# First modulations in chunks of 128 features, with norm and six open sums following chunk by chunk

## The chip, the cores and the metric

One core of one Trainium2 chip runs the whole program in a single launch. The metric is the time of one execution on the device in microseconds (us), as the median of several runs.

## What is computed

A two-layer backbone over 1024 latent tokens and 256 context tokens with 1024 features. The part of the reference that the change touches is the beginning of the first layer:

```python
for l in range(DEPTH):                                   # DEPTH = 2
    m_lat = (silu(c) @ w_mod[l] + b_mod[l])              # 6 modulations of 1024 features, latent tokens
    m_ctx = (silu(c_ctx) @ w_mod[l] + b_mod[l])          # the same for context tokens
    sh1, sc1, ga1, sh2, sc2, ga2 = split(m_lat, 6)       # shift, scale, gate; twice
    ...
    pl = modulate(rms_norm(x, g_mix[l]), sh1, sc1) @ w_in[l]       # modulate(h) = h * (1 + scale) + shift
    pc = modulate(rms_norm(ctx, g_mix[l]), csh1, csc1) @ w_in[l]
    # columns of w_in: A Mamba-2 SSD, B RG-LRU, C global attention, D windowed attention
    ...                                                  # mixers, w_out, gated residual, MLP, gated residual
```

All arithmetic is float32. Products of two large operands are made with three matmuls of split operands (high times high, high times low, low times high).

## The kernel before

**Layout.** Activations lie with features on the 128 partitions and tokens along the free axis; 1024 features are 8 tiles (k = 0 to 7). Tokens come in three groups: the 256 context tokens, latent tokens 0 to 511, and latent tokens 512 to 1023 (the third group). `h` is the normalised and modulated activation, held as a high part `hh` and a low part `hl`. `mm3` (L138) writes the three matmuls of one split product; its lines are L141, L142 and L143, whoever calls it. `act` (L133), `copy_a` (L130) and `stt` (L136) are helpers in the same way.

**The units.** A unit is one key/value head of an attention group. `unit_half` (L466) loads and splits half of its weights (8 tiles of 128 features by 256 columns; 264 for the first unit, which carries the 8 columns of the SSD's dt), and `unit_proj` (L485) makes its projection: 10 sums of 128 tokens each, 24 matmuls a sum.

**The start, in `run` (L1523).** `setup` loads constants and computes `csil`, the SiLU of both conditioning vectors, and per-layer parameters (`layer_params`, L186, which has a softplus of some 14 small VectorE instructions per layer). Then x is loaded, except the latent part of tiles 4 to 7 (the third group), and `norm_stats` (L365) squares it on ScalarE, adds the squares on VectorE, and lets TensorE sum over partitions with 2 + 4 matmuls against a column of ones. `mod_bank` (L306) computes 2048 columns of the modulations (bank 0: the first shift and scale) as one sum over 8 tiles of `w_mod`, 16 loads of 512 KB and 32 matmuls of 32 x 512, four side by side in four column groups of the array; four transposes then bring the result to feature layout. Only after the last of the 16 loads are shifts and scales known, and only then does `norm_apply` (L391) make `h`, tile by tile, and the first unit's matmuls follow.

**The rest of the layer.** `layer` (L1411) weaves generators by hand-set costs: first the unit C0 together with the third group's norm and with bank 1 of the modulations (`fill[0]`, 16 more loads of 512 KB into 3 landing buffers `e`), then attention of C0 with the first SSD projection (`p_ssd(0)`), and so on.

**What sets the order.** A scheduler places the instructions on each engine by priority (the order of the code) and by its own estimate of when an operand is ready; each engine then executes its list strictly in that order. All loads of the start are issued by one queue, SP, in order; a load into a landing buffer waits there for the last reader of that buffer, and everything behind it waits too. Landing buffers: `raw` 2, `e` 3, `u` 25 (shared with x and h).

PSUM has eight banks: `pm` 2, `qk` 3, `pt` 2, `po` 1.

## Time and profile before

| | us |
|---|---|
| median of 3 runs | 3107.39 (3104.77 to 3107.77) |
| the profiled execution | 3102.39 |
| its span, first to last instruction | 3100.6 |
| TensorE (PE) busy | 2972.3 (96% of the span) |
| VectorE (DVE) busy | 2195.9 (71%) |
| ScalarE (ACT) busy | 1516.4 (49%) |
| GpSimd (POOL) busy | 800.6 (26%) |
| mean granted TensorE clock | 0.988 |

TensorE is the engine that works nearly all the time. Its idle time is what a change can remove, and the place to look is the table of busy time by stretch: one stretch of 100 us, the first, holds more idle time of TensorE than any other. Matmuls of one engine overlap in the records (a matmul's duration includes its way through the array), so the price of one in a row of many is the distance between starts, not the duration. A float32 matmul that is not split leaves two records, a split one leaves one.

### The profile page before, as it was taken

Reading aid. Unit: us, or ns where it says so; the run is one execution under the profiler, and the core shown is the slowest. Engines: PE = TensorE matmul, PEld = TensorE weight load, DVE = VectorE, ACT = ScalarE, POOL = GpSimd, SP = SyncE. Lnnn points to the kernel's source line nnn. Section 1 sums busy time; section 2 is a strip of 40 time slices with the busy share of each in tenths; the row PEclk is TensorE's granted clock in tenths of the full one; section 3 lists DMA queues with packets and bytes.
Section 4 is the critical chain, followed back from the end, with each engine's and each line's share of the span. In section 5 each row is a group of like instructions: output and inputs, shape, how many; then the busy total and the mean of one; then the engine's idle time right before and its main releaser. Section 6 shows DMA issues by size and latency. Waiting matters only on the chain.

```text
span 3100.6 us, 45540 instructions
## 1 busy us (share of the span) xinstructions
PE 2972.3 (96%) x16210; PEld 2458.7 (79%) x16210; DVE 2195.9 (71%) x4385; ACT 1516.4 (49%) x3570; POOL 800.6 (26%) x708
## 2 busy tenths in 40 slices
PE   5998998989999999999999999999899999999999
PEld 2788887788889887788888688887788778778887
DVE  5778777787742656577777777778787886667775
ACT  4675776676544444321112577676675544442120
POOL 2214123241454100222111512223342510032220
PEclk9999998999999999999999999999999999999999
DMA  8200012330355545642222400112422564553231
GB/s 283 64 18 25 20 37 72 98 138 33 125 168 157 177 152 182 218 146 85 77 84 78 147 18 18 28 40 70 140 82 71 171 205 138 166 179 104 87 104 62
DMA packets 241076, 330.71 MB, mean 107 GB/s; under 512 B 37328, under 2 KB 159824, under 8 KB 240848
## 3 DMA queue, kind: packets, MB, share of 16 engines
q1 hardware_dynamic: 213200, 281.64, 28.5%
q10 hardware_dynamic: 27648, 46.15, 4.0%
q8 instruction: 128, 2.10, 0.3%
q14 instruction: 100, 0.82, 0.1%
HBM read 253.28 MB, written 74.45 MB: 106 GB/s over the span
## 4 chain that ended last, share of the span: by engine, by line
PE 58%; DVE 5%; ACT 4%; DMA 2%; POOL 2%; issue 2%; ACTq 0%; SPq 0%; POOLq 0%; DVEq 0%
PE qk L143 8%; PE qk L142 8%; PE qk L141 8%; PE pm L143 6%; PE pm L141 6%; PE pm L142 6%; PE pt L142 3%; PE pt L143 3%; PE pt L141 3%; PE pt L718 1%; DVE u L136 1%; PE po L727 1%; POOL wl L246 1%; PE po L728 1%; DMA u<-in_w_ffn 1%
## 5 line engine op out<-in xcount | busy, mean ns | idle before, releaser
L246 POOL TENSOR_TENSOR wl<-raw,wh 128x512 fp32r<-128x512 f32 (+1 forms) x224 | 318.8, 1437 | 1215.9 <-ACT wh L130 916.5
L141 PE MATMUL pm<-u,wh 128*128 128x512 f32 (+1 forms) x1271 | 473.8, 373 | 4.1 <-DVE u L136 2.8
L143 PE MATMUL pm<-u,wl 128*128 128x512 f32 (+1 forms) x1271 | 467.5, 368 | 1.3 <-POOL wl L246 1.3
L142 PE MATMUL pm<-u,wh 128*128 128x512 f32 (+1 forms) x1271 | 466.5, 367 | 0.0
L130 ACT ACTIVATE wh<-raw 128x512 fp32r<-128x512 f32 (+1 forms) x224 | 135.6, 628 | 484.2 <-PE qk L142 159.8
L143 PE MATMUL qk<-u,wl 128*128 128x512 f32 (+1 forms) x874 | 326.7, 374 | 1.0 <-POOL wl L246 1.0
L141 PE MATMUL qk<-u,wh 128*128 128x512 f32 (+1 forms) x874 | 324.5, 372 | 1.9 <-DVE b L1342 1.0
L130 ACT ACTIVATE s<-pt 128x512 fp32r<-128x512 f32 (+4 forms) x548 | 251.2, 467 | 120.2 <-PE pt L718 74.4
L142 PE MATMUL qk<-u,wh 128*128 128x512 f32 (+1 forms) x810 | 300.2, 371 | 2.2 <-POOL u L409 1.8
L136 DVE SCALAR_TENSOR_TENSOR u<-pm,mods,u 128x512 f32<-128x512 f32 (+1 forms) x313 | 216.5, 693 | 90.4 <-PE pm L143 89.2
L141 PEld LDWEIGHTS pm<-u,wh 128*128 128x128 f32 x1271 | 243.1, 191 | 41.2 <-DVE u L136 4.4
L143 PEld LDWEIGHTS pm<-u,wl 128*128 128x128 f32 x1271 | 242.6, 191 | 35.4 <-POOL wl L246 2.7
L142 PEld LDWEIGHTS pm<-u,wh 128*128 128x128 f32 x1271 | 243.1, 191 | 30.8
L136 DVE SCALAR_TENSOR_TENSOR u<-qk,mods,u 128x512 f32<-128x512 f32 (+1 forms) x294 | 203.7, 693 | 84.2 <-PE qk L143 83.4
L133 ACT ACTIVATE b<-b 128x512 f32<-128x512 f32 (+4 forms) x256 | 146.1, 571 | 154.6 <-DVE b L1346 123.4
L133 ACT ACTIVATE e<-qk,t 128x512 f32<-128x512 f32 (+2 forms) x336 | 188.3, 571 | 42.3 <-DVE t L651 27.2
L722 DVE TENSOR_TENSOR s<-pt,s 128x512 fp32r<-128x512 f32 (+1 forms) x256 | 166.8, 661 | 39.7 <-ACT s L130 37.2
L1394 DVE TENSOR_TENSOR u<-e,u 128x256 fp32r<-128x256 f32 (+1 forms) x160 | 160.3, 1019 | 48.8 <-ACT u L130 27.6
L141 PEld LDWEIGHTS qk<-u,wh 128*128 128x128 f32 x874 | 165.2, 189 | 34.3 <-ACT u L130 1.7
L143 PEld LDWEIGHTS qk<-u,wl 128*128 128x128 f32 x874 | 164.6, 188 | 31.7 <-POOL wl L246 1.8
L141 PE MATMUL pm<-wh,u 128*128 128x256 f32 (+1 forms) x592 | 177.8, 301 | 3.3 <-ACT b L133 1.7
L142 PEld LDWEIGHTS qk<-u,wh 128*128 128x128 f32 x810 | 152.9, 189 | 31.3 <-POOL u L409 2.7
(325 smaller groups left out, 7526.3 us busy)
## 6 DMA issues: line engine op xcount, KB each, us to landing
raw<-in_w_ffn SPq DMA_DIRECT2D x184, 256.0 KB, 2.9
e<-in_w_mod SPq DMA_DIRECT2D x64, 512.0 KB, 4.5
u<-in_w_ffn SPq DMA_DIRECT2D x60, 512.0 KB, 5.1
m<-b ACTq DMA_DIRECT2D x96, 256.0 KB, 2.0
e<-m SPq DMA_DIRECT2D x32, 640.0 KB, 4.3
u<-in_w_mod SPq DMA_DIRECT2D x32, 512.0 KB, 6.3
e<-m SPq DMA_DIRECT2D x32, 512.0 KB, 3.9
raw<-in_w_in SPq DMA_DIRECT2D x48, 256.0 KB, 2.9
```

The costliest lines, as they stand in the source:

```text
L130: return self.nc.scalar.activation(o, i, AF.Copy, **k)
L133: self.nc.scalar.activation(o, i, fn, **k)
L136: self.nc.vector.scalar_tensor_tensor(o, a, s, b, op0=op0, op1=op1)
L141: mm(o, ah, bh, start=start, stop=False, skip_group_check=part)
L142: mm(o, ah, bl, start=False, stop=False, skip_group_check=part)
L143: mm(o, al, bh, start=False, stop=stop, skip_group_check=part)
L246: self.nc.gpsimd.tensor_sub(l, raw, f(h))
L718: nc.tensor.transpose(pt[:, e * 256 + hd * P:e * 256 + hd * P + P], prs[hd][0][:, (i + e) * P:(i + e) * P + P], self.ident)
L722: nc.vector.tensor_sub(tl, pt[:, :w], f(th))
L727: nc.tensor.matmul(po[:, :256], V[:, kc, :], th[:, c], start=i + e == 0, stop=False)
L728: nc.tensor.matmul(po[:, :256], V[:, kc, :], tl[:, c], start=False, stop=i + e == len(kcs) - 1)
L1394: self.nc.vector.tensor_sub(al[:, t], raw[:, t], f(ah[:, t]))
```

## The change

1. `csil` is laid out with 32 columns per tile (two used, 30 zero), so that a slice of 32 columns holds one tile's two vectors and nothing else.
2. The weights of all units (`wu` for C0 of both layers, `wv` for the other three) are laid out by the host so that one `raw` load is one contiguous run per partition, where it was three or four strided loads.
3. The part of `w_mod[0]` for bank 0 is laid out by the host as `wm`: chunk k holds, for all 1024 inputs, the 128 shift and 128 scale columns of feature tile k (2 loads of 512 KB).
4. A new function `begin` takes the place of the start in `run`. The statistics add the squares over tiles in PSUM: 16 + 32 matmuls against the column of ones, and no adds on VectorE. For each chunk, `mod` makes 8 matmuls of 32 x 256 (inputs in four column groups, two rounds), `mod_sum` adds the four groups by 2 small matmuls against `four`, VectorE adds the bias and makes the scale, `apply` makes tile k of `h` for context and the first latent group, and `proj` adds tile k to six sums of the first unit, held open in six PSUM banks. The third group's norm (`last`) is advanced inside the same loop from chunk 4 on. Chunks 5 to 7 land in the 3 buffers `e`.
5. `unit_proj` takes these six sums and makes the remaining four itself.
6. Most of `layer_params` moves from `setup` to the point behind the first weave of layer 0.

```diff
+        for k in range(3):
+            load(k)
+        rss = [stats(*g) for g in G_ALL[:2]]
+        rb = {g[0]: rows(g[1], rs) for g, rs in zip(G_ALL[:2], rss)}
+        nt = (CTX + 512) // P
+        self.sums = [self.PS(t)[:, :WU] for t in ("pm", "pm", "qk", "qk", "qk", "po")]
...
+        rest = last()
+        for k in range(KD):
+            if k + 3 < KD:
+                load(k + 3)
+            if k == 1:
+                for i in range(4, KD):
+                    nc.sync.dma_start(x.tiles[i][:, 0:1024], xt[i][:, 0:1024])
+            sb = mod(k)
+            if k >= 2:
+                proj(k - 2)
+            mod_sum(k, sb)
+            for g in G_ALL[:2]:
+                apply(k, *g)
+            if k >= 4:
+                for _ in range(5):
+                    next(rest, None)
...
+        proj(KD - 2)
+        proj(KD - 1)
...
+            for kk in range(KD):
+                cg = kk % 4
+                mm(ps[32 * cg:32 * cg + 32, 0:256], self.csil[:, 32 * kk:32 * kk + 32],
+                   land[k][kk // 4][:, 256 * cg:256 * cg + 256], start=kk < 4, stop=kk >= 4, skip_group_check=True,
+                   tile_position=(0, 32 * cg))
...
+            for k in range(KD):
+                sq, xk = self.S(n), x.at(k, t0, n)
+                if k % 2:
+                    nc.vector.tensor_mul(sq, xk, xk)
+                else:
+                    self.act(sq, xk, AF.Square)
+                for j in range(nt):
+                    mm(pss[:, j:j + 1], sq[:, j * P:(j + 1) * P], self.one, start=False, stop=k == KD - 1,
+                       skip_group_check=True)
...
+        def proj(k):
+            wh, wl = ws[k // 4]
+            for tt in range(nt):
+                self.mm3(self.sums[tt], hh.at(k, tt * P, P), hl.at(k, tt * P, P), wh[:, k % 4], wl[:, k % 4],
+                         k == 0, k == KD - 1, True)
...
         def loads(r, i):
...
+            c = (4 * kh + 2 * i) * nw
+            return [(r, w[:, c:c + 2 * nw])]
```

**TensorE at the start.** In these rows `pt`, `po`, `pm` and `qk` are PSUM banks, `one` is the column of ones, `s` a square or a copied modulation, `rnd` the identity, `csil` the conditioning, `u` and `e` landing buffers of `w_mod`, and `wh`, `wl` the split weights. Before:

```order
L384 MATMUL pt<-one,s 128x1 x2
L319 MATMUL po<-u,csil 32x512
L384 MATMUL pt<-one,s 128x1 x4
L319 MATMUL po<-u,csil 32x512 x3
L400 MATMUL pt<-rnd,t 128x128 x4
L319 MATMUL po<-u,csil 32x512 x2
L400 MATMUL pt<-rnd,t 128x128 x2
L319 MATMUL po<-u,csil 32x512 x26
L328 MATMUL po<-rnd,b 128x128 x4
L141 MATMUL pm<-wh,u 128x264
```

And now (L1568 statistics, L1551 transposes, L1580 `mod`, L1590 `mod_sum`):

```order
L1560 MATMUL pt<-csil,rnd 128x2
L1560 MATMUL pt<-csil,rnd 128x4
L1568 MATMUL pt<-one,s 128x1 x28
L1551 MATMUL pt<-rnd,t 128x128 x2
L1568 MATMUL pt<-one,s 128x1 x20
L1551 MATMUL pt<-rnd,t 128x128 x4
L1580 MATMUL pt<-u,csil 32x256 x8
L1590 MATMUL pt<-four,s 128x2 x2
L1580 MATMUL pt<-u,csil 32x256 x8
L1590 MATMUL pt<-four,s 128x2 x2
L1580 MATMUL pt<-u,csil 32x256 x8
L141 MATMUL pm<-wh,u 128x264
```

The matmuls of the first unit now stand behind three chunks instead of behind all 32 matmuls of the bank, and 48 statistics matmuls stand ahead of the first chunk, where there were 6 in two places.

**TensorE around the third group's norm.** Before, the statistics and transposes of the third group (L384, L400) stood among the unit's sums, behind eleven matmuls of bank 1 (L319):

```order
L319 MATMUL po<-e,csil 32x512 x11
L141 MATMUL pm<-wh,u 128x264
...
L143 MATMUL pm<-wh,u 128x264
L384 MATMUL pt<-one,s 128x1 x4
L141 MATMUL pm<-wh,u 128x264
```

Now, from chunk 5 on (the first row is its `mod`; the fifth row ends its `proj`):

```order
L1580 MATMUL pt<-e,csil 32x256 x8
L1590 MATMUL pt<-four,s 128x2 x2
L141 MATMUL pm<-wh,u 128x264
...
L143 MATMUL po<-wh,u 128x264
L392 MATMUL pt<-one,s 128x1 x4
L1551 MATMUL pt<-rnd,t 128x128 x4
L1580 MATMUL pt<-e,csil 32x256 x8
L1590 MATMUL pt<-four,s 128x2 x2
L1580 MATMUL pt<-e,csil 32x256 x4
L141 MATMUL pm<-wh,u 128x264
```

In chunks 5, 6 and 7 nothing of another chunk's `proj` stands between a `mod` and the `proj` of the same chunk, where chunks 0 to 4 run ahead by one or two; and the third group's statistics and transposes stand between `proj` of chunk 5 and `mod` of chunk 6.

**VectorE in chunks 6 and 7.** `mods` and `ms` are shift and scale, `s<-u,ms,b` is the multiplication that starts `apply`, and `u<-s,mods,u` the low part of `h`. Before, the whole bank's shifts and scales were made at once, and `norm_apply` followed:

```order
L333 TENSOR_TENSOR mods_244<-po,pp_94 128x16 x2
L136 SCALAR_TENSOR_TENSOR ms_245<-mods_244,pp_94 128x8 x2
L136 SCALAR_TENSOR_TENSOR s<-u,ms_245,pt 128x256 x3
L136 SCALAR_TENSOR_TENSOR u<-s,mods_244,u 128x256
L136 SCALAR_TENSOR_TENSOR s<-u,ms_245,pt 128x256 x3
```

Now, from the shift and scale of chunk 6 to the end of chunk 7:

```order
L1593 TENSOR_TENSOR mods_116<-pt,pp_96 128x2x2
L1594 TENSOR_SCALAR ms_117<-mods_116,pp_96 128x2
L136 SCALAR_TENSOR_TENSOR s<-u,ms_117,b 128x256
L136 SCALAR_TENSOR_TENSOR s<-u,ms_117,b 128x512
...
L136 SCALAR_TENSOR_TENSOR s<-u,ms_117,b 128x512 x3
L136 SCALAR_TENSOR_TENSOR u<-s,mods_116,u 128x512
L1593 TENSOR_TENSOR mods_116<-pt,pp_96 128x2x2
L1594 TENSOR_SCALAR ms_117<-mods_116,pp_96 128x2
L136 SCALAR_TENSOR_TENSOR u<-s,mods_116,u 128x512
L136 SCALAR_TENSOR_TENSOR s<-u,ms_117,b 128x256
L136 SCALAR_TENSOR_TENSOR s<-u,ms_117,b 128x512 x4
```

Eleven instructions of `apply` stand between the scale of chunk 6 and the shift of chunk 7: four are chunk 6's own for the first two groups, seven the third group's (five of the first kind, two of the second). The rows left out are five of the eleven: one `u` of 128x256, two `s` and two `u` of 128x512.

## Rows read from the trace of the kernel before

**Rows 1.** Busy time by stretches of 100 us, all engines, clock, DMA share, GB/s

```profile
0.00:100.00 100.00, 68.65 (x373) 38.66 (x374) 57.60 (x155) 45.99 (x105) 31.92 (x30) 0.97 0.74 251
100.00:200.00 100.00, 97.09 (x599) 81.53 (x599) 77.01 (x201) 72.28 (x194) 17.42 (x18) 1.00 0.11 26
```

**Rows 2.** Busy time by stretches of the start, same columns

```profile
0.00:42.40 42.40, 19.18 (x78) 5.85 (x78) 15.19 (x59) 12.66 (x27) 8.14 (x10) 1.00 0.92 318
46.40:75.00 28.60, 23.04 (x109) 12.87 (x110) 19.76 (x35) 18.98 (x40) 13.58 (x12) 0.88 0.74 238
75.00:115.60 40.60, 39.09 (x273) 31.14 (x272) 33.59 (x94) 19.29 (x52) 17.14 (x14) 1.00 0.35 104
```

**Rows 3.** PE's timeline: start, duration, operation, idle time before it and its end

```profile
23.11 1.87 PE L384 MATMUL pt<-one,s 128*128 128x1 f32 x8 [2.22 <-DVE s L380]
42.41 1.05 PE L319 MATMUL po<-u,csil 128*32 128x512 f32 x4 [0.23 <-DMA u<-in_w_mod]
46.42 0.39 PE L141 MATMUL pm<-wh,u 128*128 128x264 f32 x1 [1.60 <-ACT u L406]
71.88 0.95 PE L384 MATMUL pt<-one,s 128*128 128x1 f32 x8
74.17 0.65 PE L400 MATMUL pt<-rnd,t 128*128 128x128 f32 x4 [0.74 <-POOL t L388]
78.64 0.39 PE L141 MATMUL pm<-wh,u 128*128 128x264 f32 x1
81.75 1.05 PE L319 MATMUL po<-e,csil 128*32 128x512 f32 x2
85.83 1.06 PE L319 MATMUL po<-e,csil 128*32 128x512 f32 x8
106.56 0.66 PE L328 MATMUL po<-rnd,b 128*128 128x128 f32 x4
108.01 0.39 PE L141 MATMUL pm<-u,wh 128*128 128x512 f32 x1
112.18 0.38 PE L609 MATMUL qk<-rnd,b 128*128 128x128 f32 x2
115.20 0.44 PE L609 MATMUL qk<-rnd,b 128*128 128x128 f32 x2 [1.23 <-DVE b L604]
115.61 0.48 PE L141 MATMUL pm<-u,wh 128*128 128x512 f32 x1
```

**Rows 4.** Timelines of ACT, DVE and POOL in the start, same columns

```profile
7.71 0.42 ACT L133 ACTIVATE s<-u 128x256 f32<-128x256 f32 x1 [2.02 <-DMA u<-in_xt]
12.50 6.11 ACT L133 ACTIVATE s<-u 128x256 f32<-128x256 f32 x13 [1.21 <-DMA u<-in_xt]
58.89 0.72 ACT L406 ACTIVATE u<-s,mods 128x512 fp32r<-128x512 f32 x1
45.34 1.26 DVE L136 SCALAR_TENSOR_TENSOR s<-u,ms,pt 128x256 f32<-128x256 f32 x3
50.33 1.40 DVE L136 SCALAR_TENSOR_TENSOR s<-u,ms,pt 128x512 f32<-128x512 f32 x2
55.06 1.16 DVE L136 SCALAR_TENSOR_TENSOR u<-s,mods,u 128x512 fp32r<-128x512 f32 x1
57.45 0.74 DVE L136 SCALAR_TENSOR_TENSOR u<-s,mods,u 128x512 fp32r<-128x512 f32 x1
16.71 1.08 POOL L388 TENSOR_TENSOR t<-t,mhalf 128x2 f32<-128x2 f32 x1 [16.27 <-DVE t L386]
61.85 1.26 POOL L409 TENSOR_TENSOR u<-s,u 128x512 fp32r<-128x512 f32 x1
```

**Rows 5.** One microsecond of PE: busy, instructions, granted clock, DMA share, GB/s

```profile
50.00:51.00 1.00, 1.00 (x7) 0.50 1.01 389
```

**Rows 6.** What PE waited for, 580 to 620 us: total, times, longest

```profile
PE pm L142 <- POOL wl L246: 2.5, 2, 2.2
```

**Rows 7.** DMA issues of the page: count, KB each, median us from issue to landing

```profile
e<-in_w_mod SPq DMA_DIRECT2D x64, 512.0 KB, 4.5
```

More of the change, by code (lines that the diff above doesn't have):

```diff
@@ L172, in setup @@
         nc.vector.tensor_scalar(ch, cT, 0.5, None, op0=ALU.mult)
-        self.csil = self.const([P, 2 * KD + 30], "csil")
+        self.csil = self.const([P, 32 * KD], "csil")
         nc.vector.memset(self.csil, 0.0)
-        self.stt(self.csil[:, 0:2 * KD].rearrange("p (k j) -> p k j", j=2), th, 1.0, ch, ALU.add, ALU.mult)
-        self.L = [self.layer_params(l) for l in range(DEPTH)]
+        self.stt(self.csil.rearrange("p (k j) -> p k j", j=32)[:, :, 0:2], th, 1.0, ch, ALU.add, ALU.mult)
+        self.four = self.const([P, 2], "four")
+        nc.vector.tensor_reduce(self.four, self.ident.rearrange("p (g r) -> p r g", g=4)[:, 0:2], axis=AX.X, op=ALU.add)
+        self.L = []
+        for l in range(DEPTH):
+            pp = self.const([P, NPP], f"pp{l}")
+            nc.sync.dma_start(pp, self.I["pp"][l])
+            self.L.append({"pp": pp})
     def late_setup(self):
@@ L187, in layer_params @@
         nc = self.nc
[L188 to L191 removed]
+        p = self.L[l]
+        pp = p["pp"]
         hp = self.const([P, 40], f"hp{l}")
@@ L318, in mod_bank @@
             for cg in range(4):
-                nc.tensor.matmul(ps[32 * cg:32 * cg + 32, :], self.csil[:, 2 * k:2 * k + 32],
+                nc.tensor.matmul(ps[32 * cg:32 * cg + 32, :], self.csil[:, 32 * k:32 * k + 32],
                                  raws[cg // 2][:, 512 * (cg % 2):512 * (cg % 2) + 512],
@@ L333, in mod_bank, with mod_tiles @@
             nc.vector.tensor_add(m[:, 16 * b:16 * b + 16, st].rearrange("p (c q) -> p c q", c=4), v[:, :, :, st], bm)
+    def mod_tiles(self, l):
+        p = self.L[l]
+        p["mods"] = self.const([P, 48, 2], f"mods{l}")
+        p["s"] = [self.const([P, 8, 2], f"ms{l}{i}") for i in range(2)]
     def mods(self, l, banks, land, tag="po"):
@@ L338, in mods @@
         if "mods" not in p:
-            p["mods"] = self.const([P, 48, 2], f"mods{l}")
-            p["s"] = [self.const([P, 8, 2], f"ms{l}{i}") for i in range(2)]
+            self.mod_tiles(l)
         for b in banks:
@@ L517, in unit_proj @@
                 t0 = tt * P
-                if (0 if t0 < CTX else CTX + (t0 - CTX) // 512 * 512) not in hh.done:
+                if tt >= len(sums) and (0 if t0 < CTX else CTX + (t0 - CTX) // 512 * 512) not in hh.done:
                     yield from hh.pending
-                ps = self.PS()[:, :nw] if with_dt else ps2[:, a * 256:a * 256 + 256]
-                for k in range(KD):
+                if tt < len(sums):
+                    ps = sums[tt]
+                else:
+                    ps = self.PS()[:, :nw] if with_dt else ps2[:, a * 256:a * 256 + 256]
+                for k in range(KD if tt >= len(sums) else 0):
                     wh, wl = ws[k // 4]
@@ L1423, in p_attn @@
             ws = self.first if with_dt else self.next_weights(2)
-            un[kind, kv] = yield from self.unit_proj(l, h, ws, rr, with_dt, need_ctx)
+            un[kind, kv] = yield from self.unit_proj(l, h, ws, rr, with_dt, need_ctx,
+                                                     self.sums if with_dt and l == 0 else ())
         def m_attn(kind, kv):
@@ L1466, in layer @@
         self.x = None
+        for i in range(DEPTH if l == 0 else 0):
+            self.layer_params(i)
         ps0, dt = p_ssd(0), self.ssd_dt(l)
@@ L1532, in run @@
             self.nc.sync.dma_start(x.tiles[i][:, t], xt[i][:, t])
-        rs = {}
-        def stats(t0, n):
-            rs[t0] = yield from self.norm_stats(self.x, t0, n, False)
-        for g in G_ALL[:2]:
-            drain(stats(*g))
-        self.first = [self.unit_half(0, W_AC, 0, 0, True)]
-        mods = self.mods(0, [0], self.U)
-        drain(take(mods, 6.0))
-        self.first.append(self.unit_half(0, W_AC, 0, 1, True))
-        drain(take(mods, 9.0))
-        for i in range(4, KD):
-            self.nc.sync.dma_start(x.tiles[i][:, 0:1024], xt[i][:, 0:1024])
-        drain(mods)
-        self.late_setup()
-        h = self.new_h()
-        def norm(i):
-            yield from self.norm_apply(0, 0, x, h, *G_ALL[i], rs[G_ALL[i][0]])
-        def last():
-            yield from stats(*G_ALL[2])
-            yield from norm(2)
-        drain(norm(0))
-        drain(norm(1))
-        self.next = h, last()
+        self.next = self.begin(x, xt)
         for l in range(DEPTH):
```

100 lines of the change are left out of this document (81 added, 19 removed).

## The prediction

> **What bounds the kernel now.** I read the table of busy time by stretches of 100 us first. TensorE is busy for 68.65 us of the first 100 and for 97.09 of the next [rows 1]; the gain, if there is one, lies in the first stretch. Cut where its work changes, that stretch shows three states [rows 2]. Up to 42.4 us the DMA engines are busy for 92% at 318 GB/s and TensorE for 19.18 us: it waits for bank 0 of the modulations, whose last matmuls start at 42.41, and the unit's first matmul follows at 46.42 [rows 3]. From 46.4 to 75 TensorE is busy for 23.04 of 28.6 us, at a mean clock of 0.88. From 75 to 115.6 it is busy for 39.09 of 40.6 us: there nothing but less work would help. So the change can only use idle time ahead of 46.4, where six of the unit's ten sums would fit.
>
> To compare, I take a mark that both kernels pass: the start of the 49th matmul of the first SSD projection (24 of 256 columns and 24 of 512 stand ahead of it). Before, it starts at 115.61 [rows 3], with the ten sums, all of bank 1 and its transposes done. The time the changed kernel needs to the same mark, less 115.6, is the change at the start.
>
> **The change part by part.**
>
> *Statistics.* They turn from 6 matmuls into 48. Four such matmuls (eight records) took 0.95 us at 71.88 but 1.87 at 23.11 [rows 3], where TensorE had hardly worked before: 0.24 against 0.47 us each, the two clock levels (2.4 and 1.2 GHz). The first square ends at 8.1 (7.71 + 0.42), and the 13 squares from 12.50 on show that by then the tiles are there [rows 4]. I take the 16 context matmuls at 0.47 and the arrival of tiles together to end at 17, and the other 32 at 0.24: 17 + 7.7 = 24.7. The ends are 22 (all at 0.24 from the last context square on) and 31 (8.1 + 48 x 0.47). The power on POOL (1.08, [rows 4]), some 0.3 around it, an estimate, and four transposes (0.65, [rows 3]) put `mod` of chunk 0 at 27. These 48 matmuls are the hidden cost of the change: before, the adds lay on VectorE under the transfers, now TensorE's list has them ahead of every chunk.
>
> *Chunks 0 to 4.* A `mod` has four column groups side by side, two rounds of half the columns: like the eight records of 85.83, 1.06 us. `mod_sum` loads 128 columns of weights twice, like two statistics matmuls: 0.48. `proj` has 18 matmuls; 24 took from 78.64 to 81.75, 0.13 each, so 2.3 [rows 3]. Chunk 0 has to pass through ScalarE and VectorE before its `proj` can end: copy 0.42, `mod_sum` 0.48, shift and scale 0.3 (an estimate), multiplications 0.42 and 0.70, high part 0.72, the same front of chunk 1 on VectorE and then the low parts, 0.48 and 0.74 (the 256-column one an estimate, between 0.42 and 0.74) [rows 4]: `proj` of chunk 0 ends at about 34. From there TensorE's list is full: four more `proj` (9.2), three `mod` (3.2) and three `mod_sum` (1.4) end `mod` of chunk 5 at 47.8. Its data are no obstacle: constants, x, unit weights and six chunks are 13.1 MB, at 318 GB/s [rows 2] 41 us.
>
> *Chunks 5 to 7.* Here the order leaves TensorE nothing to run ahead with. From `mod` of chunk 5: 0.42 + 0.48 + 0.3 + 0.42 + 0.70, then on the odd tiles two passes of ScalarE (0.72 each), one of POOL (1.26) and the last four matmuls (0.5): 5.5 us, 53.3. Behind it in the list the third group's statistics (0.95), power (1.08 + 0.3) and transposes (0.65): 56.3. `mod` of chunk 6, copy and `mod_sum`: 58.3. On VectorE eleven instructions now stand ahead of the shift of chunk 7: six multiplications of 512 columns (0.70), three low parts (0.74), and 0.42 + 0.48 of 256 columns [rows 4], with the scales before and after 7.9 us: 66.2. One more low part and two multiplications (1.9), then ScalarE twice, POOL and four matmuls as above (3.2): 71.3, with hand-overs 72 for the end of the six sums. The last load of chunk 7 stands on SP behind a weight load that waits for POOL; issued at 58 and taking 4.5 us [rows 7] it lands before 66, hidden by VectorE's list; if POOL were later by more than 3 us, it would show.
>
> *From there to the mark.* Four sums, 4 x 3.1 = 12.4. Bank 1: the order has it as one group of three and one of one, two of four and ten of two matmuls; a group of two alone took 1.05 and of four 1.06, a single one 1.05 [rows 3], so 14 groups or 14.7 us. It is dearer than the eight groups that four at a time would be, since it is cut into halves. Small SSD matmuls at most 24 x 0.13 = 3.1; large ones 0.232 each (18 from 108.01 to 112.18), 5.6; bank transposes 0.66; five pairs of small transposes (0.38 each) 1.9 [rows 3]. Together 38.4. The waits of TensorE in this stretch lie between 0 and 4; the 1.23 at 115.20 is the nearest row, I take 2.
>
> *The clock.* After the gapped work up to 46.4 the clock stood at 0.50 between 50 and 51 [rows 5]. Chunks 5 to 7 have more gaps: 11 us of matmuls in 24. At half clock their chain would be longer by 0.9 (statistics), 0.7 (transposes), 1.1 (`mod`), 0.5 (`mod_sum`), 0.5 (last four): 3.7; and one further sum at half clock costs 3.1. Between 0 and 6.8, I take 2, since the longest piece is VectorE's.
>
> *Sum.* 72 + 38.4 + 2 + 2 = 114.4 against 115.6: 1.2 us gained, out of 31 idle. VectorE beside POOL can be slower (1.16 for the low part that else takes 0.74, [rows 4]): up to 2 us, part of the range.
>
> *The rest.* The moved parameters are some 32 VectorE instructions of 128x4, 5 us together, into a stretch where VectorE is busy for 77 of 100 us [rows 1]: 0 to 3, I take 1. Contiguous unit weights move the same bytes with fewer issues; TensorE waited for a unit's split weights for 2.5 us near 600 [rows 6], but on POOL, which does the same work: 0 to 2.5, I take 1 gained. The zeros in `csil`, the smaller x at the start and the host's layouts cost nothing on a path. That the change would not overlap at all is excluded by the order of TensorE, in which `proj` stands among the chunks.
>
> The profiled execution would come to 3102.4 - 1.2 = 3101.2, and the median of the runs shown is 5.0 above it: **3106.2, say 3106**.
>
> **The rivals.**
>
> *Chunks 5 to 7 at TensorE's pace* (faster). If VectorE gets through the third group's instructions while TensorE is still in chunks 4 and 5, each chunk costs only its matmuls: 47.8 + 2.3 + 3.0 + two times 3.84, and a tail of 4 or so: 64 to 65 instead of 72, which gives 3098 to 3099; with the statistics at full clock throughout (22 instead of 24.7) 3096. For it: VectorE has only some 28 us of work between 27 and 72. Against: its list is strict, and the eleven instructions come behind the scale of chunk 6. Chance 0.3.
>
> *The clock stays low* (slower). If the statistics run at 1.2 GHz to their end (32 x 0.23 = 7.4 later) and chunks 5 to 7 too (6.8 instead of 2), the six sums end at 84 and the mark is passed at 126.6, 11 us late: 3118. It decides from the point at which the six sums end 2 us behind my 72 (then nothing is gained), and shows in a measurement from 80 on. For it: rows at 23.11 and between 50 and 51. Against: 48 matmuls in a row are more work than anything before 27 in the old kernel. The Trainium skill, "TensorE: Matmul & The Clock Gate", section "HAM oscillation — how this bites in real kernels", tells of a kernel whose bursts of matmuls were shorter than the waits between them and which fell back to half clock at every step; by that rule chunks 5 to 7 run at half clock, and the time would be near this rival's 3112 to 3118. The trace agrees so far as the clock did fall after gapped work, for a few us. Chance 0.2.
>
> **How the numbers follow.** About 6 us (0.2%) is what a measurement can tell from no change. The forecast, within that, has 0.5; its own range is 3101 to 3112 from the ends of the waits, clock and contention. Faster by over 0.2% has 0.3 (3096 to 3099), slower 0.2 (to 3118). Leaving out half of the slower case and some of the faster: 3094 to 3114.
>
> **What would show it.** In the profile after: the statistics' last matmul near 25 at 0.24 us each; `mod` of chunk 5 near 47; three gaps of several us on TensorE before the `proj` of chunks 5, 6 and 7, the last ended by POOL, with VectorE busy in front of the shift of chunk 7; the six sums done near 72; the mark near 114. If the sums end near 64 the faster rival holds; if the clock reads 0.50 through most of 50 to 80 and the sums end past 80, the slower one. A difference at other places than the first 130 us of over 4 us would make the sum wrong, whatever the total.

## The result

The changed kernel takes 3127.47 us (median of 4, 3124.99 to 3128.08), the kernel before, on the same chip, 3106.41 (median of 4): a ratio of 1.0067, 95% interval 1.0049 to 1.0084, or 21.1 us slower. The forecast was 3106, no change, with a range to 3114; the slower rival, priced at 3118, had the right sign and was still 9 us short. The profiled execution of after took 3128.08 (span 3126.3, mean granted clock 0.984).

**By stretch.** In the busy time by stretches of after (PE, PEld, DVE, ACT, POOL, clock, DMA share, GB/s), the first row answers to [rows 1]; the second is the whole way to the mark, and then come the stages, cut where the work changes: to the end of the statistics, of chunk 0's `proj`, to `mod` of chunk 5, to the end of the six sums, to the mark.

```profile
0.00:100.00 100.00, 75.98 (x457) 61.83 (x458) 44.48 (x90) 44.91 (x96) 32.40 (x31) 0.88 0.54 187
...
0.00:133.00 133.00, 107.20 (x635) 80.44 (x635) 63.78 (x162) 52.19 (x118) 39.24 (x36) 0.91 0.57 189
0.00:31.40 31.40, 22.45 (x102) 22.02 (x102) 5.56 (x20) 7.30 (x14) 4.50 (x8) 1.00 0.76 261
31.40:46.15 14.75, 12.77 (x82) 8.44 (x82) 5.46 (x10) 6.17 (x12) 5.40 (x5) 1.00 0.93 373
46.15:59.00 12.85, 12.67 (x117) 10.90 (x120) 8.45 (x17) 7.74 (x15) 2.49 (x3) 1.00 0.00 1
59.00:93.20 34.20, 22.51 (x127) 16.94 (x127) 21.33 (x30) 18.58 (x35) 15.41 (x14) 0.65 0.44 134
93.20:133.00 39.80, 36.80 (x213) 22.14 (x213) 22.98 (x86) 12.40 (x43) 11.44 (x9) 1.00 0.57 172
```

And the way to the mark in before:

```profile
0.00:115.60 115.60, 83.02 (x466) 50.42 (x467) 70.05 (x193) 52.07 (x121) 38.86 (x35) 0.97 0.68 226
```

The mark is passed 17.3 us late. But TensorE is idle for 25.8 us ahead of it (133.0 - 107.2), where it was idle for 32.6 before (115.6 - 83.0). So 6.8 us of idle time are filled. But TensorE is also busy for 24.2 us longer, for the same projections: 42 more statistics matmuls at 0.43 us each (below) are 18 of them. What fills the idle time is mostly work that was not there before; that is the first thing to explain.

TensorE's timeline of after (start, duration, operation, idle time before it and what ended it):

```profile
12.57 9.55 PE L1568 MATMUL pt<-one,s 128*128 128x1 f32 x44 [0.64 <-DVE s L1564]
22.43 8.53 PE L1568 MATMUL pt<-one,s 128*128 128x1 f32 x40
33.36 1.94 PE L1580 MATMUL pt<-u,csil 128*32 128x256 f32 x16
46.15 1.07 PE L1580 MATMUL pt<-u,csil 128*32 128x256 f32 x16
58.93 1.07 PE L1580 MATMUL pt<-e,csil 128*32 128x256 f32 x16
63.57 0.59 PE L141 MATMUL pm<-wh,u 128*128 128x264 f32 x1 [2.40 <-ACT u L133]
88.02 0.59 PE L141 MATMUL pm<-wh,u 128*128 128x264 f32 x1 [4.26 <-ACT u L133]
93.18 0.39 PE L141 MATMUL pm<-wh,u 128*128 128x264 f32 x1 [0.17 <-ACT dtr L130]
132.95 0.47 PE L141 MATMUL pm<-u,wh 128*128 128x512 f32 x1
149.62 0.48 PE L720 MATMUL pt<-rnd,e 128*128 128x128 f32 x1 [4.51 <-ACT e L133]
```

Two records are one statistics matmul, so 44 records in 9.55 us are 0.43 us each, and the last 40 as well: half rate to the end, at 31, with TensorE busy without a gap. `mod` takes 1.94 us up to chunk 2 and 1.07 from 46.15 on. From 59 to 93 the mean clock is 0.65. The last row is a wait of 4.51 us behind the mark, where [rows 3] has ended; in the trace of before the longest wait of TensorE from 120 to 160 us is 0.25.

### The profile page after: what moved, and what is told of

The parts are those of the page before. It is cut to its first block, busy times and chain, and to the rows that moved or that the text cites. A ratio compares the mean times of both kernels' runs of the same rounds, so it can differ in the third digit from the quotient of the medians.

```text
span 3126.3 us, 45754 instructions
## 1 busy us (share of the span) xinstructions
PE 2999.5 (96%) x16390; PEld 2494.4 (80%) x16390; DVE 2190.6 (70%) x4389; ACT 1521.1 (49%) x3572; POOL 798.4 (26%) x711
## 3 DMA queue, kind: packets, MB, share of 16 engines
q10 hardware_dynamic: 27648, 46.15, 3.9%
## 4 chain that ended last, share of the span: by engine, by line
PE 57%; DVE 6%; ACT 3%; DMA 2%; issue 2%; POOL 2%; SPq 0%; ACTq 0%; POOLq 0%; DVEq 0%
PE qk L141 8%; PE qk L143 8%; PE qk L142 8%; PE pm L143 6%; PE pm L141 6%; PE pm L142 6%; PE pt L142 3%; PE pt L143 3%; PE pt L141 3%; DVE u L136 1%; PE pt L720 1%; PE po L729 1%; PE po L730 1%; DMA raw<-in_w_ffn 1%; PE po L323 1%
## 5 line engine op out<-in xcount | busy, mean ns | idle before, releaser
L143 PEld LDWEIGHTS qk<-u,wl 128*128 128x128 f32 x874 | 164.8, 189 | 32.1 <-POOL wl L250 2.0
L142 PEld LDWEIGHTS qk<-u,wh 128*128 128x128 f32 x810 | 153.2, 189 | 30.4 <-POOL u L417 1.6
L141 PE MATMUL pm<-wh,u 128*128 128x256 f32 (+1 forms) x560 | 168.4, 302 | 7.8 <-ACT u L133 7.7
```

The source lines that it names most:

```text
L141: mm(o, ah, bh, start=start, stop=False, skip_group_check=part)
L142: mm(o, ah, bl, start=False, stop=False, skip_group_check=part)
L143: mm(o, al, bh, start=False, stop=stop, skip_group_check=part)
```

## Theories and experiments

Theory A: the start is late because the statistics and the chunks run at half clock and because the third group's norm stands in the way of chunks 6 and 7; the wait at 149.62 comes from the moved parameters. Rivals: the transfers bind the start; the price of a one-column matmul is not the clock's; the reordered rest costs the time. Each kernel is compared with the kernel before as it ran beside it on the same chip (medians 3107.34, 3105.84, 3104.77 and 3105.71 for the four groups of kernels); after stood 21.1 above its own. The intervals of these ratios are some 0.1 to 0.2% to either side, 3 to 5 us, so a difference between two changed kernels that is smaller than that rests on the traces and not on the medians.

### Parameters back in setup

```diff
+        for l in range(DEPTH):
+            self.layer_params(l)
...
-        for i in range(DEPTH if l == 0 else 0):
-            self.layer_params(i)
```

> The softplus and the other per-layer parameters are made in setup again, as before the change; all else is the changed kernel, and TensorE's order is the same. In the changed kernel TensorE waits 4.51 us at 149.62 in the attention of C0, while VectorE works through some 32 instructions of 128x4. Theory A (the moved parameters cost this wait): the wait falls under 1 us, the six sums still end near 93 and the mark stays at 133 within 1.5 us; the time falls by 3 to 5 us, to about 3123. Theory B (that wait belongs to the reordered rest and only changes place): within 1 us of 3127. If the small VectorE instructions delay csil and the squares at the start, the mark comes up to 2 us later and part of the gain is lost.

Measured: 3118.92, 11.6 above before (ratio 1.0041, 1.0026 to 1.0056): 9.5 us of the 21 belong to the moved parameters (8.55 if the medians of after and of this kernel are compared as they stand), about twice what was expected, though the mark comes 1.5 us later (134.46). Behind the mark the profiled execution takes 2993.4 us in after and 2983.3 here (span less mark), and the wait of 4.51 us is gone. The stretch from 140 to 150 in after, then the same in this kernel:

```profile
140.00:150.00 10.00, 5.49 (x33) 4.70 (x32) 8.02 (x27) 3.35 (x11) 4.29 (x4) 0.88 0.39 106
```

```profile
140.00:150.00 10.00, 9.79 (x59) 7.99 (x58) 5.48 (x16) 8.46 (x26) 3.97 (x5) 1.00 0.22 55
```

How a few small instructions do this is in the timelines of after (ScalarE, then VectorE):

```profile
136.38 0.60 ACT L130 ACTIVATE b<-po 128x512 f32<-128x512 f32 x1 [1.31 <-PE po L323]
136.88 0.20 ACT L133 ACTIVATE b<-t 128x4 f32<-128x4 f32 x1
...
137.47 0.17 DVE L228 TENSOR_SCALAR b<-b 128x4 f32<-128x4 f32 x1 [13.34 <-ACT b L133]
...
148.03 0.68 DVE L690 TENSOR_REDUCE t<-qk 128x2 f32<-128x512 f32 x1
```

The softplus begins on ScalarE (absolute value, exponential) and goes on on VectorE. ScalarE's strict list has its first two steps behind the copy of bank 1's result, which TensorE delivers at 136. VectorE's list has the softplus ahead of the first reduction of C0's attention (L690), so VectorE waits 13.34 us for four columns, works through two softplus chains, and reduces at 148.03 scores whose matmuls were issued by 138.7. TensorE idles 4.5 us, and from 150 to 160 its mean clock is 0.78.

### Statistics with adds on VectorE

```diff
-        rss = [stats(*g) for g in G_ALL[:2]]
+        rss = [value(self.norm_stats(x, *g, False)) for g in G_ALL[:2]]
```

> Only the statistics of the first two groups go back to the old way: squares on ScalarE, adds on VectorE, 6 matmuls against the column of ones on TensorE instead of 48. The order behind is unchanged. Theory A (48 statistics matmuls at half clock delay every chunk): the last statistics matmul starts near 24 instead of 30, mod of chunk 0 near 28 instead of 33.4, the six sums end 5 to 6 us earlier (87 to 88), the time falls by about 6 to 3121; the first three chunks are still at half clock (mod 1.9 us). Theory B (the start is bound by the transfers of chunks and weights): mod of chunk 0 comes earlier but mod of chunk 5 stays at 58 to 59; less than 2 us gained.

(`value` runs the generator to its end and returns its result.) Measured: 3121.47, 14.1 above before (1.0049, 1.0032 to 1.0066), so 7.0 less than after (6.0 with the medians as they stand); the two intervals overlap, but the mark too comes 5.0 us earlier, at 127.99. TensorE's timeline of this kernel: statistics, first `mod`, `mod` of chunk 5, first matmul behind the six sums.

```profile
25.71 1.87 PE L392 MATMUL pt<-one,s 128*128 128x1 f32 x8 [8.34 <-DVE s L388]
...
29.97 1.94 PE L1580 MATMUL pt<-u,csil 128*32 128x256 f32 x16
...
54.59 1.07 PE L1580 MATMUL pt<-e,csil 128*32 128x256 f32 x16
...
88.03 0.39 PE L141 MATMUL pm<-wh,u 128*128 128x264 f32 x1 [0.28 <-ACT dtr L130]
```

The statistics end at 27.58 (25.71 + 1.87), where they ended at 30.96 in after, and the other three rows stood at 33.36, 58.93 and 93.18: everything moves by 3.4 to 5.2 us. `mod` of chunk 5 moves by 4.3, so the transfers didn't hold it. To the mark TensorE is now busy for 86.1 us instead of 107.2, and idle for 41.9 instead of 25.8: the idle time that the change had filled was filled by its statistics, and with the adds on VectorE the chunks leave TensorE more idle than it was before (32.6). The stretch to the mark in this kernel:

```profile
0.00:127.99 127.99, 86.08 (x546) 59.18 (x547) 67.97 (x168) 55.67 (x126) 39.45 (x36) 0.93 0.60 196
```

### Wide matmuls beside the statistics

```diff
+        wide = self.PS("po")
+        for _ in range(16):
+            mm(wide, self.identr, self.rnd, start=True, stop=True)
...
+                for _ in range(2):
+                    mm(wide[:, :n], self.identr, sr, start=True, stop=True)
```

> Adds work to the changed kernel that nobody reads: 16 matmuls of 128x512 (fp32r) while TensorE waits for x, and two wide matmuls of each square (256 or 512 columns) ahead of its statistics; squares are rounded to fp32r. Nothing is taken away. Theory A (the one-column matmuls don't raise the granted clock, wide ones do): the statistics take 0.24 us each instead of 0.45, though TensorE has 32 more matmuls among them; they end at 26 to 28 instead of 31, the first mods take 1.06 instead of 1.94, proj of chunk 0 ends near 37 to 39 instead of 45.7, and the time falls by 6 to 9 us to 3118 to 3121. Theory B (0.45 us is the price of such a matmul here, whatever the clock): they stay at 0.43 or more, the wide ones come on top at 0.2 to 0.4 each, the statistics end past 38 and the time is 3134 to 3138.

Measured: 3133.22, 25.9 above before (1.0087, 1.0071 to 1.0103): just under the time of theory B. The rows say otherwise about the cause. Timeline, then two stretches of this kernel:

```profile
4.23 6.75 PE L1631 MATMUL po<-rnd 128*128 128x512 f32 x16 [4.23 <-ACT rnd L130]
...
11.28 0.50 PE L1572 MATMUL pt<-one,s 128*128 128x1 f32 x4
...
24.91 1.70 PE L1572 MATMUL pt<-one,s 128*128 128x1 f32 x8
```

```profile
10.80:17.20 6.40, 6.40 (x55) 6.29 (x54) 2.25 (x6) 4.35 (x9) 0.14 (x1) 0.99 0.97 358
17.20:36.70 19.50, 19.50 (x79) 18.12 (x78) 1.58 (x3) 0.05 (x1) 4.00 (x3) 0.50 0.78 272
```

Behind the 16 wide matmuls the same two statistics matmuls take 0.50 us together, 0.25 each, at a granted clock of 0.99; from 17.2 on they take 0.43 each at 0.50, though TensorE is busy all the time in both stretches. So the price is the clock's, against theory B; but what I added did not hold the clock up, against theory A's time, and cost 1.0 us for each square of 512 tokens besides.

### Third group left to the layer

```diff
-            if k >= 4:
-                for _ in range(5):
-                    next(rest, None)
```

> The third group's norm is no longer advanced inside the chunk loop; it is left to the weave of the layer, as before the change. All else is the changed kernel. Theory A (from chunk 5 on the third group's statistics, transposes and multiplications stand in the way of chunks 6 and 7): mod of chunk 5 stays at 59, the six sums end at 76 to 80 instead of 93, part is given back where the third group's norm is needed for the last four sums; the time falls by 7 to 13, to about 3117. Theory B (chunks 6 and 7 wait for their landing buffers e, each freed by the mod before): the sums still end past 86 and the time falls by less than 4.

Measured: 3130.67, 23.3 above before (1.0079, 1.0064 to 1.0094). Theory A was right in direction on the six sums, which end at 74.8 instead of 93 (76 to 80 were expected), and wrong on the time, which was to fall by 7 to 13 us. Timeline of TensorE behind the sums:

```profile
80.03 1.91 PE L323 MATMUL po<-e,csil 128*32 128x512 f32 x2 [5.21 <-ACT dtr L130]
...
90.12 0.69 PE L611 MATMUL qk<-rnd,b 128*128 128x128 f32 x2 [4.47 <-DVE b L606]
```

Bank 1 waits for bank `po` to be emptied of the sixth sum, the transposes wait for VectorE, and the pieces between run at half clock: 1.91 us for one matmul (two records), where one took 1.05 in [rows 3]. The mark is passed at 138.5.

### Contiguous unit weights alone, in the kernel before

```diff
-            ls = [(r[:, :, 0:128], src(base + 128 * kv, 128)),
-                  (r[:, :, 128:192], src(base + 256 + 64 * kv, 64)),
-                  (r[:, :, 192:256], src(base + 384 + 64 * kv, 64))]
...
+            return [(r, w[:, c:c + 2 * nw])]
```

> The kernel before with one part of the change alone: the weights of the units laid out contiguously, one load where there were three or four. Theory A (the same bytes; the splits on ScalarE and POOL bound a unit's weights, not the loads): 3105 to 3108, within 2.5 us of before. Rival (fewer issues on SP let loads start earlier, or the scheduler's estimates place the rest otherwise): 3 us or more to either side; what it differs by would then belong to the 20 us of the change.

Measured: 3096.42, 9.4 below before (0.9971, 0.9960 to 0.9981). A second time, beside the kernels with five sums further down:

> The kernel before with contiguous unit weights a second time, on the same chip as the two kernels with five sums, to compare with them. By the first time: 3096 within 3 us, 8 to 11 below before. If it comes out within 4 us of before, the first gain was of that chip or that day.

Measured: 3098.22, 7.5 below (0.9972, 0.9963 to 0.9982). This part alone is the fastest kernel of the study, below both. One stretch of before and of this kernel (the last two columns are DMA share and GB/s):

```profile
22.00:30.00 8.00, 6.89 (x32) 3.36 (x36) 1.21 (x2) 0.00 (x0) 1.52 (x2) 1.00 0.99 337
```

```profile
22.00:30.00 8.00, 7.33 (x38) 3.73 (x42) 0.78 (x2) 1.28 (x2) 3.66 (x4) 1.00 1.03 407
```

The timelines: issues of the unit's first weights on SP in before; the same in this kernel, and the unit's first matmul.

```profile
7.70 7.21 SPq L258 DMA_DIRECT2D raw<-in_w_in  x8
```

```profile
7.31 1.91 SPq L258 DMA_DIRECT2D raw<-in_wu  x2
...
41.64 0.39 PE L141 MATMUL pm<-wh,u 128*128 128x264 f32 x1 [1.61 <-ACT u L406]
```

The DMA engines were as busy with the strided loads (0.99) as without (1.03), but moved 337 instead of 407 GB/s, and SP issued for 7.2 instead of 1.9 us. The unit starts 4.8 us earlier (41.64 against 46.42), the mark 2.5 (113.14). The strided pieces are 512, 256 and, for the 8 columns of dt, 32 bytes long. In the packet records of the trace of before, between 22 and 30 us, a packet of 256 bytes took 18 ns on average, one of 512 bytes 32 and one of 4096 bytes 166: 14, 16 and 25 GB/s on one DMA engine. The Trainium skill, "DMA: Bandwidth & Descriptors", section "Specifications", gives 512 bytes as the least transfer for full rate; the trace agrees as far as the rate rose by a fifth when the short pieces went, but not on the limit, since the pieces of 512 bytes still moved at two thirds of the rate of the long ones. The two profiled executions differ by 2.6 us where the medians differ by 9.4. Behind the mark they take 2985.0 us in before and 2984.9 and 2983.9 in the two traces with contiguous weights (span less mark), so where the rest of the gain lies isn't shown.

### Both parts undone, and two additions to that

```diff
+            self.layer_params(l)
...
+        rss = [value(self.norm_stats(x, *g, False)) for g in G_ALL[:2]]
```

> Two parts undone together: the parameters are made in setup, and the statistics add on VectorE with 6 matmuls. Alone they gave 8.5 and 6.0 us. Theory A (one is a wait at the attention of C0, the other stands ahead of all chunks, so they don't meet): the gains add up, 3112 to 3115. Rival (both act through the same idle time): 3117 or more. In both cases it stays slower than before, by the chunks at half clock and the chain of chunks 5 to 7.

Measured: 3111.62, 5.8 above before (1.0020, 1.0011 to 1.0030). The sum of the two was 21.1 - 9.5 - 7.0 = 4.6: they add up. Against contiguous weights in the kernel before, what is left of the change, the chunks, still loses 13.3 to 15.2 us. This takes it that contiguous weights gain as much beside the chunks as alone; no run has the chunks with the old loads, so that is not shown. Busy time up to 29.3, near chunk 0's `mod`, and from there to the mark, in this kernel and then in the one with contiguous weights:

```profile
0.00:29.30 29.30, 4.68 (x22) 3.84 (x26) 16.72 (x60) 12.97 (x29) 7.46 (x10) 1.00 0.83 279
...
29.30:128.50 99.20, 83.25 (x529) 56.48 (x521) 57.01 (x141) 43.53 (x102) 31.25 (x26) 0.88 0.51 170
```

```profile
0.00:29.30 29.30, 10.84 (x42) 4.88 (x46) 15.13 (x59) 12.61 (x27) 7.46 (x10) 1.00 0.95 357
29.30:113.10 83.80, 71.84 (x427) 47.11 (x420) 54.76 (x134) 39.41 (x94) 31.52 (x26) 0.94 0.56 187
```

To the mark TensorE is busy for 87.9 us and idle for 40.6 with chunks, busy for 82.7 and idle for 30.4 without. The chunks were to use idle time; with the statistics taken out again, there is 10 us more of it, and half-rate matmuls on top (clock 0.88 against 0.94).

Landing chunks 5 to 7 in `u`:

```diff
-                raw = (self.U if k < 5 else self.E)()[:, 0:1024]
+                raw = self.U()[:, 0:1024]
```

> As the kernel with both parts undone, and chunks 5 to 7 land in buffers u like the others instead of the three e; the order on TensorE has mod of chunk 5 ahead of proj of chunk 4, and both halves of mod 7 ahead of proj 6. Theory A (chunks 5 to 7 are held by the third group's norm: VectorE's eleven instructions, POOL's power, the half clock): chunk 5's wait goes but the six sums end only 3 to 5 us earlier, near 83; 2 to 5 us less than with e. Rival (landing in e is what holds them): the sums end near 76, 8 or more us less.

Measured: 3113.32, 7.5 above before (1.0029, 1.0017 to 1.0041), no better than with `e`. The six sums end near 92, behind the 88.8 with `e`: `mod` of chunk 5 comes earlier, but the wait ahead of the last chunk's `proj` is 4.20 us as it was 4.27. The landing buffers were not what held the chunks; the 3 to 5 us that theory A expected did not come either.

Wide matmuls while TensorE is idle ahead of chunk 0:

```diff
+        for _ in range(28):
+            mm(wide, self.identr, self.first[0][0][:, 0:512], start=True, stop=True)
```

> As the kernel with both parts undone, and 28 matmuls of 128x512 (fp32r) that nobody reads, on TensorE while it waits for the adds (20) and for the power (8), in time in which it is idle. Theory A (wide matmuls raise the granted clock, and the first chunks then start at full clock): the 28 start at 0.43 us each and end at 0.22; the first mods take 1.07 us instead of 1.94, proj of chunk 0 ends 3 to 5 us earlier, and the time is 3 to 5 us below that of the kernel without them. Rival (the clock falls again in the gaps between the statistics, the transposes and mod, or they delay the statistics): mods at 1.9 us and no gain, or up to 2 us slower.

Measured: 3111.69, 5.9 above before (1.0021, 1.0011 to 1.0030). Timeline:

```profile
15.89 6.52 PE L1634 MATMUL po<-wh,rnd 128*128 128x512 f32 x20
...
29.54 1.12 PE L1580 MATMUL pt<-u,csil 128*32 128x256 f32 x16
...
85.55 0.39 PE L141 MATMUL pm<-wh,u 128*128 128x264 f32 x1 [0.59 <-ACT dtr L130]
```

The mechanism is as expected: the first `mod` takes 1.12 us instead of 1.94, the six sums end 3.2 us earlier and the mark is passed 3.2 us earlier (125.32 against 128.50). The median of ten runs doesn't move. Where 3 us are given back behind the mark is open; the profiled execution (3104.73) was the fastest of the ten.

### The third group behind chunk 7

These three kernels have the parameters in setup, the adds on VectorE, the 28 wide matmuls, all chunks in `u`, and the sum in `po` as the first of the six; they differ in where the third group's norm is advanced (the first is shown; the second takes 20 steps behind chunk 7, the third five steps each in chunks 6 and 7):

```diff
-            if k >= 4:
-                for _ in range(5):
+            if k == 7:
+                for _ in range(10):
                     next(rest, None)
```

> All that the runs so far point at, together: parameters in setup, adds on VectorE, the 28 wide matmuls ahead of chunk 0, chunks 5 to 7 landing in u; the third group is touched only behind chunk 7 (its statistics and power there, its multiplications in the weave of the layer), and the sum in bank po is the first of the six, so that bank 1 of the modulations can start sooner. Theory A (what is left of the 15 us by which the chunks lose against the kernel before with contiguous weights is the third group's norm between the chunks): all eight chunks run at TensorE's 3.9 us, the six sums end at 62 to 68, the mark is passed at 104 to 109 against 113.1, the time is 3088 to 3094. Rival (the third group's norm is only put off: TensorE waits for it or for VectorE behind the six sums, as where it was left to the layer alone): the sums end near 66, but the mark is not before 116, the time 3100 to 3112.

Measured: 3112.76, 8.0 above before (1.0016, 1.0002 to 1.0030). The six sums end at 67.4, 26 us earlier than in after and 17.6 earlier than in the kernel with the wide matmuls (84.96), as theory A had it; the mark is passed at 128.92, as the rival had it. TensorE behind the sums, and the queue SP:

```profile
73.50 1.84 PE L394 MATMUL pt<-one,s 128*128 128x1 f32 x8 [6.13 <-DVE s L390]
...
78.84 1.92 PE L325 MATMUL po<-e,csil 128*32 128x512 f32 x2 [1.03 <-ACT dtr L130]
...
46.90 3.04 SPq L321 DMA_DIRECT2D e<-in_w_mod  x3
...
83.38 21.59 SPq L321 DMA_DIRECT2D e<-in_w_mod  x10
```

Bank 1's first three loads are issued at 46.9 and lie in their buffers until 78.84; the next ten can be issued only from 83.38 on. Meanwhile TensorE waits 6.13 us for the third group's squares and then starts again at half clock.

> As the one with the third group behind chunk 7, but its multiplications also stand ahead of the unit's rope on VectorE and ScalarE, so that the last four sums come before the transposes of the first six on TensorE. Theory A: sums end at 62 to 68, the last four sums follow from about 78 with bank 1 between, the mark at 104 to 109, 3088 to 3094, at or below the kernel where only its statistics are there. Rival (TensorE waits for the third group's tiles one after the other): a wait of 5 us or more ahead of the last four sums, the mark at 112 or later, 3098 to 3106.

Measured: 3111.17, 6.4 above before (1.0014, 1.0003 to 1.0025); mark at 128.05.

> As the one with the third group behind chunk 7, but its statistics start with chunk 6 (five steps each in chunks 6 and 7), so that its squares use ScalarE's and POOL's idle time there. Theory A: the six sums end 1 to 3 us later than with the statistics behind chunk 7 (VectorE's adds stand in the way of chunk 7), the third group's transposes 3 us earlier; the time is within 3 us of that kernel. Rival (any of the third group's work between the chunks costs its full price): the sums end past 72 and the time is 4 us or more above it.

Measured: 3110.96, 6.2 above before (1.0015, 1.0001 to 1.0030); mark at 124.44. Three places for the third group, one time within their intervals, and none near the 3088 to 3094 of theory A: that the third group between the chunks costs the time fell. It can be moved out of their way, and then stands in the way of what follows.

### Five open sums instead of six

New theory: what covered the third group's norm before was the first unit itself and bank 1 beside it. The chunks run the six sums ahead of it, and six open sums hold every PSUM bank but the two that the chunks use, so bank 1 cannot take their place.

```diff
-        self.sums = [self.PS(t)[:, :WU] for t in ("po", "pm", "pm", "qk", "qk", "qk")]
+        self.sums = [self.PS(t)[:, :WU] for t in ("pm", "pm", "qk", "qk", "qk")]
```

> As the one whose third group starts in chunks 6 and 7, but only five sums stay open through the chunks (128 tokens less), so that bank po is free and bank 1 of the modulations can run beside the chunks; the other five sums follow. Theory A (six open sums hold all banks but the two of the chunks, so TensorE has nothing to run in their gaps and in the third group's norm, while bank 1's first three loads lie in their buffers): bank 1's first matmuls start before 62 instead of 79, TensorE's wait ahead of the third group's statistics falls under 3 us, the mark is passed at 112 to 118 instead of 124 to 129, the time is 3096 to 3104. Rival (the gaps are VectorE's and ScalarE's own chain, filled or not): the mark stays past 122 and the time at 3108 to 3113.

Measured: 3107.80, 2.1 above before, not to be told from it (1.0005, 0.9996 to 1.0014). Timeline of the first bank 1 matmuls and of what follows:

```profile
64.04 1.05 PE L325 MATMUL po<-e,csil 128*32 128x512 f32 x4
67.83 0.59 PE L141 MATMUL pm<-wh,u 128*128 128x264 f32 x1 [2.75 <-ACT u L133]
```

The kernel to compare is the third of the last three, with six sums, where these rows stand:

```profile
72.27 1.84 PE L394 MATMUL pt<-one,s 128*128 128x1 f32 x8 [1.25 <-DVE s L390]
...
77.60 3.62 PE L325 MATMUL po<-e,csil 128*32 128x512 f32 x10 [1.03 <-ACT dtr L130]
```

With five, bank 1 starts at 64.04 instead of 77.60, TensorE no longer waits ahead of the third group's statistics (1.25 there), and the mark comes at 121.87, 2.6 us earlier. The time is 4.1 lower, each to its own before, but the two intervals overlap, so the medians don't show the gain. The direction is the theory's; the size falls short of it (mark 112 to 118, time 3096 to 3104) and close to its rival (past 122, 3108 to 3113).

> The same five open sums with the third group advanced where the changed kernel has it, five steps in each of chunks 4 to 7. TensorE's list now has eleven groups of bank 1 around chunk 7, but none between chunk 5 and the third group's transposes. Theory A (free bank): the wait of 4.3 us ahead of chunk 7's matmuls is filled, the mark at 114 to 121, the time 3098 to 3107, a few us above the one with the third group in chunks 6 and 7. Rival: as with six sums, mark near 125 to 129, 3110 to 3114.

Measured: 3111.18, 5.5 above before (1.0016, 1.0006 to 1.0026); mark at 129.96. With the third group between the chunks, its transposes stand ahead of all of bank 1 in TensorE's list, and the free bank helps nothing. So the order in the traces supports the free bank as a part of the cause in one arrangement out of two, and the times show it in neither. About 10 us between the best kernel with chunks (3107.80) and the kernel before with contiguous weights beside it (3098.22) stay unexplained in detail.

## Why the prediction was wrong, step by step

The order of events was right; three terms of the sum were not: the price of a statistics matmul (0.24 us taken for 32 of the 48, 0.43 or more measured for every one), the half clock in chunk 0 and in chunks 5 to 7 (nothing and 2 us taken), and the moved parameters (1 us taken, 9.5 measured).

| step | forecast | after |
|---|---|---|
| statistics end | 24.7 (22 to 31) | 31.0 |
| `proj` of chunk 0 ends | 34 | 45.7 |
| `mod` of chunk 5 starts | 46.7 | 58.9 |
| six sums end | 74, with 2 for the clock | 93.0 |
| from there to the mark | 40.4, with 2 of waits | 40.0 |
| mark | 114.4 | 132.95 |
| moved parameters | +1 (0 to 3) | +9.5 |
| contiguous weights | -1 (0 to -2.5) | -7.5 and -9.4, alone |

**Statistics.** Of the two prices I had, 0.24 and 0.47, I took the first for 32 of 48 matmuls, because TensorE would by then have worked for long. The row for 0.24, at 71.88 in [rows 3], stands among matmuls of 264 columns; the row for 0.47 stands among gaps, as this stage does. The upper end of my own bound, 31, is what came; that it fits to the tenth is luck, since the matmuls took 0.43 and not 0.47, and waits for x made up the rest. The step that failed is the choice between the ends: `mod` of chunk 0 starts at 33.4 instead of 27.

**Chunk 0.** Its `proj` ends 11.7 us late; the 5.3 us that the statistics don't explain are the same error again. Three `mod` and two `mod_sum` stand ahead of chunk 0's `proj` and ran at half clock, and so did most of that `proj`; I had costed them at 1.06 and 0.48.

**Chunks 0 to 4.** Forecast 12.7 from the end of chunk 0's `proj` to `mod` of chunk 5, measured 13.2. At full clock the list was priced rightly, and the data were no obstacle.

**Chunks 5 to 7.** Forecast 27.3 us with the clock, from `mod` of chunk 5 to the end of the sums, measured 34.1. The order of events was as told: three waits (2.40 ahead of chunk 5, 1.01 ahead of chunk 6, 4.26 ahead of chunk 7, each ended by ScalarE; I had POOL for the last), VectorE's eleven instructions from 77.17 to 84.96 (7.8 against 7.9), and the last load of chunk 7 hidden behind them. The clock was mis-sized: I took 2 of a bound of 6.8, and the mean granted clock from 59 to 93.2 is 0.65. The bound was too small as well, since all of it gives 32.1. It charged half clock to the last four matmuls of a `proj`; all 18 of chunk 5 (63.57 to 68.14) and of chunk 7 (88.02 to 93.01) ran behind their waits at a granted clock of 0.50 and 0.51 (in after):

```profile
63.57:68.14 4.57, 4.57 (x18) 4.09 (x18) 1.49 (x2) 3.68 (x8) 3.27 (x3) 0.50 0.82 246
88.02:93.01 4.99, 4.86 (x18) 4.14 (x18) 3.94 (x5) 4.99 (x10) 3.28 (x3) 0.51 0.00 0
```

Row 50:51 of [rows 5] was at hand and I read it as a dip of a few us. The Trainium skill's section "HAM oscillation — how this bites in real kernels" ("TensorE: Matmul & The Clock Gate"), which I had put into the slower rival, tells of bursts of matmuls shorter than the waits between them, each of which starts at half clock. The trace agrees on what comes of it, with that 0.65, and not on the condition: the two bursts of 4.6 and 5.0 us were longer than the waits of 2.40 and 4.26 ahead of them.

What the half clock costs in time is worked out from rows. The one kernel that took it away, in the first chunks, passed the mark 3.2 us earlier without a lower median, so no run shows that price in the whole time.

**To the mark.** 40.0 against 40.4: the four sums, bank 1 in half groups and the SSD matmuls were priced well.

**Parameters.** I summed the instructions (5 us) and asked how busy VectorE is. The price was a chain: ScalarE's list, then VectorE's list, with the attention's first reduction behind it. I had not named what is queued behind the moved instructions on either engine.

**Contiguous weights.** I wrote "the same bytes", and priced the data at the 318 GB/s that stand beside a DMA share of 92% [rows 2], as if that were the rate to be had. A busy share doesn't tell a rate: with contiguous weights the engines moved 357 GB/s up to 29.3 us, at a share of 95%.

**Outside the start.** I said that a difference elsewhere of over 4 us would make the sum wrong, whatever the total. It was: the parameters against me, the weights for me, and they nearly cancelled.

The medians add up: parameters +9.5, statistics +7.0, the chunks +13.3 to +15.2 and, as much less, the contiguous weights -7.5 to -9.4 give 22.3; measured were 21.1. The weights cancel in this sum, because the chunks were taken as a difference to them; what it tests is that the first two parts and the 5.8 us left without them make up the whole.

## What to carry to other kernels

Filling an engine's idle time was worth nothing here, where what filled it was added work at half clock and the pieces that were moved had covered the next stage: price a moved piece by the rows around the place it goes to, and ask what covers the stage that it leaves. Small instructions that cross two engines can cost what stands behind them on both lists, here 9.5 us for 5 us of their own time. Split a change into its parts on the chip: here the plainest part alone beat the kernel before, while the whole lost.

## What was not expected of the hardware

- Statistics matmuls (one column against 128 columns of weights) ran for 18.4 us with hardly a gap, from 12.57 to 31, and were at half rate from the first to the last. The same ones ran at full rate in the 6.4 us behind 16 matmuls of 512 columns, and fell back while TensorE stayed fully busy.
- The clock column read 1.00 for the first 31.4 us of after, while the durations there were those of half rate: ahead of the first change that is recorded, durations tell the level, the column doesn't.
- DMA engines that read 0.99 busy moved 337 GB/s with strided pieces of 32 to 512 bytes among the loads, and 407 without.
- Runs of one kernel on one chip differed by up to 17 us (the kernel before, 3101.40 to 3118.41 in 25; the one with parameters and adds undone, 3106.83 to 3117.76 in ten), and 3 us at the mark were not found again in a median.
